# A bidirectional recurrence on one Trainium2 core: norms of the next unit in a thread of their own, block inverses of both directions merged together

## The chip, the cores and the metric

The kernel runs on one core of one Trainium2 chip. The metric is the device time of one execution in microseconds (us), lower is better. The kernel before takes 1797.82 us (median of 3 runs, 1797.66 to 1800.14).

## The reference

A small encoder trunk of one layer is applied to two requests (batches b = 0 and 1) of 512 tokens and 1024 features, in float32. The layer adds to x the sum of two gated branches, A (a bidirectional RWKV-7 recurrence of 8 heads of 64) and B (a latent attention of 8 heads), and then a SwiGLU block; a norm ends it. What the change touches is branch A, and in it the recurrence and the unit norm of kk:

```python
def _rwkv7_scan(r, w, k, v, kk, a, reverse):
    ...
    def step(state, inp):
        r_t, w_t, k_t, v_t, kk_t, a_t = inp
        sa = jnp.einsum('bhvk,bhk->bhv', state, kk_t)
        state = (state * w_t[:, :, None, :]
                 - sa[..., None] * (kk_t * a_t)[:, :, None, :]
                 + v_t[..., None] * k_t[:, :, None, :])
        return state, jnp.einsum('bhvk,bhk->bhv', state, r_t)
...
def _rwkv7_branch(p, w2, w0, a2, a0, g2, k_k, k_a, r_k, gn_g, gn_b):
    ...
    kk = heads(pk * k_k)
    kk = kk / jnp.maximum(jnp.sqrt(jnp.sum(kk * kk, axis=-1, keepdims=True)), 1e-12)
    ...
    o = (_rwkv7_scan(r, heads(wf), heads(kf), v, kk, heads(af), reverse=False)
         + _rwkv7_scan(r, heads(wb), heads(kb), v, kk, heads(ab), reverse=True))
    ...
    bonus = jnp.sum(r * heads(pk) * r_k, axis=-1, keepdims=True) * v
    return (o + bonus.reshape(bsz, s, A_WIDTH)) * g
```

The two requests share all weights.

## The kernel before

The recurrence isn't run token by token. The tokens are cut into 8 chunks of 64 (NCH, CH), and the work into 8 units: one per batch and pair of heads, in the order of `order` (pair 0 of batch 0, pair 0 of batch 1, pair 1 of batch 0 and so on). A unit treats both directions (NI = 2, the backward one on reversed tokens) and passes these steps:

- **prep**, first half (L822 and following): loads r, k and v in one tile (x3, L826), scales k to kk (L829), squares it (L831), sums the squares per head by a product (`row_stats`), takes the power -1/2 on POOL (L838, rn), spreads the result by `bcast_rows` (an ACT copy and four transposes) and forms nkk, the negated unit vectors (L842), and the bonus bo (L844 to L849, with the product bp). These are the norms. Then for each direction it loads decay and rate (c_, a_), scans, and forms pp, bt and kt.
- **prep**, second half: waits until the state run two units earlier is issued (`yield free`, since its buffers exist for two units), forms ka and kb, the products gx (L893, L894) and their masked copies nt and arb (L897, L898), and stores nt to HBM. It calls **lanes**, then makes the products gy and three groups of transposes per direction (tb, tk, vp).
- **lanes** (L938 to L971): inverts the 32x32 diagonal blocks of all chunks, heads and directions at once, by 31 dependent steps of a multiply (L963, lt) and an add (L965, el) on POOL, from a tile `lane` that is read back from HBM. The result goes to HBM (e_d).
- **merge** (L974 to L1004): joins the 32-blocks to 64-blocks. For each direction it loads e and ntl, transposes (L988, tp), multiplies (zp), copies (L995, z), multiplies (xp) and copies into e (L1003). The second direction follows the first.
- **state** (L1006): 8 dependent chunk steps, each with the products s1, s2 and s3 and between them copies to rs (L1033, DVE), sva (L1052, ACT), svb (L1053, DVE) and sums (L1060, L1061).
- **post** (L1066): copies o out (L1072), normalizes per head and stores y.

The order of TensorE's instructions is written by `drive`: threads of generators, each with an offset that is its priority. `drive` always resumes the first thread in the list that is due, and adds the modelled cost of its matmuls to a clock, `pe["now"]`. A yielded number asks for a pause of that many us of TensorE's clock, times SLACK (or SLS for the state thread); a yielded function waits until it is true. The offset is also the priority by which the other engines' instructions are ordered. The threads, first to last, are state, post, merge, prep, fill and combine. The prep thread does the units one after the other; merge i waits for a due time, TL us after lanes i was issued. Fill is the work that takes what is left of TensorE: the projections of r, k and v for the later pairs (pj_rkv), the gates (pj_gt, pj_gtl), and then the whole attention (sc, pt, pav, kps, qps, vps). Combine of batch 0 (pab) starts when all units and the attention of batch 0 are through. After that come the output projection, the combine of batch 1 and the SwiGLU block.

The short names of rows: lt and el are lanes, tp, z and zp, xp are merge, s is any of s1 to s3.

Of the kernel before, what the change touches and what calls it, by code (L numbers as in the profile page):

```python
# [18 lines left out]
P = 128  # L19
# [25 lines left out]
TL = 40  # L45
SLACK = 1.4
SLS = 1.2
# [12 lines left out]
YG = 0.75  # L60
YT = 1.43
YT2 = 0.85
YM1 = 2
YM2 = 1.1
YO1 = 1.3
# [3 lines left out]
YQ = 2.27  # L69
YK = 1.71  # L70
OFFS = 200000, 150000, 120000, 100000, 0, 0
# [9 lines left out]
PL = 4.06  # L81
# [26 lines left out]
def trunk(ctx, tc, outs, x, w_in, w2, g2, w_uq, w_ukk, w_ukv, w_oab, w_out, w_gu, w_down,  # L108
# [76 lines left out]
    def bcast_rows(sp, pp, rn, nh, name, rbtag):  # L185
# [624 lines left out]
    class Unit:  # L810
# [8 lines left out]
        def tmp(self, name):  # L819
            return rp0.tile([P, S], F32, tag="tmp", bufs=NT, name=f"{name}{self.nm}")  # L820

        def prep(self, free):  # L822
            b, p, nm, tmp = self.b, self.p, self.nm, self.tmp
            kra, krb, arb, bka, bkb = [], [], [], [], []
            x3 = rp0.tile([P, 3, S], F32, tag="rkv", bufs=1, name=f"rkv{nm}")
            nc.sync.dma_start(x3, rwkv_in[b][p][:, 0:3])  # L826
            r_, k_, v_ = x3[:, 0], x3[:, 1], x3[:, 2]
            kk = tmp("kk")
            nc.scalar.activation(kk, k_, AF.Copy, scale=cc(C_KK + p))  # L829
# [4 lines left out]
            ss = row_stats(_MG(), sq, 2, f"kk{nm}")  # L834
# [4 lines left out]
            rb = bcast_rows(rp0, _MG(), rn, 2, f"kk{nm}", ("tmp", NT))  # L839
            yield YP3  # L840
            nkk = rp0.tile([P, S], F32, tag="nkk", bufs=1, name=f"nkk{nm}")
            nc.vector.scalar_tensor_tensor(out=nkk, in0=kk, scalar=-1.0, in1=rb, op0=ALU.mult, op1=ALU.mult)  # L842
            bo = tmp("bo")
            nc.vector.scalar_tensor_tensor(out=bo, in0=r_, scalar=cc(C_RK + p), in1=k_, op0=ALU.mult, op1=ALU.mult)  # L844
            bp = mg(f"bp{nm}")
            mm(bp, b64, bo)
            yield YP4
            nc.vector.tensor_mul(bo, bp, v_)
            nc.sync.dma_start(bo_d[b][p], bo)  # L849
            halves = []  # L850
# [27 lines left out]
            for d, (rev, pp_, bt_, kt_) in enumerate(halves):  # L878
# [24 lines left out]
                kra.append(ka_), krb.append(kb_), arb.append(rb_)  # L903
            self.lanes()
# [69 lines left out]
        def merge(self):  # L974
            nm = self.nm
            nt, ed = nt_d[self.par], e_d[self.par]
            self.ee = []
            for i in range(NI):
                e_ = rp.tile([P, NCH, CH], F32, tag="e", bufs=4, name=f"e{nm}{i}")

                def tmp3(name):
                    return rp.tile([P, NCH, 32], F32, tag=name, bufs=1, name=f"{name}{nm}{i}")
                tp, ntl, z_ = tmp3("tp"), tmp3("ntl"), tmp3("z")
                for h, hs in enumerate((HA, HB)):
                    q = slice((i * 2 + h) * NCH, (i * 2 + h + 1) * NCH)
                    nc.sync.dma_start(ntl[Q[2 * h]], nt[q, 0:32, 32:].rearrange("c r t -> r c t"))
                    nc.sync.dma_start(e_[hs], ed[q].rearrange("c r t -> r c t"))
                nc.vector.transpose(tp, e_[:, :, 0:32])  # L988
                zp = mg(f"zp{nm}{i}").rearrange("p (c t) -> p c t", t=32)
                for c in range(NCH):  # L990
                    for h in range(2):
                        mm(zp[Q[2 * h + 1], c], ntl[Q[2 * h], c], tp[Q[2 * h], c], tile_position=(h * 64, h * 64 + 32))
                yield YM1
                for h in range(2):
                    (nc.scalar.copy, nc.vector.tensor_copy)[h](z_[Q[2 * h + 1]], zp[Q[2 * h + 1], 0:NCH])  # L995
                xp_ = mg(f"xp{nm}{i}").rearrange("p (c t) -> p c t", t=32)
                for c in range(NCH):
                    for h in range(2):
                        mm(xp_[Q[2 * h], c], z_[Q[2 * h + 1], c], e_[Q[2 * h + 1], c, 32:],
                           tile_position=(h * 64 + 32, h * 64))  # L1000
                yield YM2
                for h in range(2):
                    (nc.scalar.copy, nc.vector.tensor_copy)[h](e_[Q[2 * h], :, 32:], xp_[Q[2 * h], 0:NCH])  # L1003
                self.ee.append(e_)  # L1004
# [89 lines left out]
    def has(*k):  # L1094
        return lambda: k in done

    preps = [u.prep(has("state", i - 2) if i > 1 else 0 if i else "rp") for i, u in enumerate(units)]

    def first_prep():
        for r in preps[0]:  # L1100
            if r == "rp":
                return
            yield r
# [122 lines left out]
    drive(list(zip(OFFS, (state_thread(), post_thread(), merge_thread(), prep_thread(), fill_thread(),  # L1226
# [618 lines left out]
```

## Time and profile before

| | |
|---|---|
| runs | 1797.82 us median, 1797.66 to 1800.14 (3 runs) |
| the profiled execution | 1794.72 us |
| its span | 1792.9 us |
| mean granted TensorE clock | 0.985 |

The span goes from the first to the last instruction of the one profiled execution. Busy time is the time in which an engine worked (DMA issues and waits aren't counted); the idle time of an engine is followed by what ended it. PE is TensorE's matmuls, PEld its weight loads, which run beside them; DVE, ACT and POOL are the vector, scalar and general engines, SP issues most DMAs. In a stretch's row stand its bounds, its length, and for each engine the busy us and the instructions in it, then the granted clock of TensorE (1.00 is full speed), the share of the DMA engines and GB/s. In a row of waits stand the waiting instruction, the one it waited for, the total, the number of waits and the longest. Matmuls of an fp32 product are recorded as two passes, so that their count is twice that in the code.

### The profile page before, as it was taken

To read this page: it belongs to the slowest core of one execution; us is meant where nothing else is said; L and a number is where in the kernel's file an instruction comes from. 1 tells how busy PE (TensorE), PEld (TensorE's weight loads), DVE (VectorE), ACT (ScalarE), POOL (GpSimd) and SP (SyncE) were. 2 spreads that over 40 slices of the span, in tenths; PEclk is the share of its full clock that TensorE was granted. 3 is DMA by queue.
4 is the path that set the end of the run, shared out by engine and by line. 5 is a ranking of instruction groups with operands and counts; after the bars stand their busy time and mean duration, and the time that the engine had idled before them with its cause. 6 is when DMAs were issued, how large, how long until landed. Compare 5 with 4: busy or idle time off the path is not lost.

```text
span 1792.9 us, 30793 instructions
## 1 busy us (share of the span) xinstructions
PE 1706.5 (95%) x11660; PEld 1350.2 (75%) x11660; DVE 1076.8 (60%) x1781; ACT 786.1 (44%) x1525; POOL 625.9 (35%) x984
## 2 busy tenths in 40 slices
PE   7999999999999997999999999699999999989997
PEld 6778767777777775666667988488888888868886
DVE  6734564636445365855566657865565565498757
ACT  6743424344433336676663324333333333245445
POOL 1121536364553636260012126733343333200006
PEclk9999999999999998999999999799999999999999
DMA  5473343434334344211367531123222222283442
GB/s 179 140 254 100 114 112 81 128 92 119 114 85 121 86 113 118 73 39 34 129 200 265 177 114 36 36 87 107 94 90 99 83 88 77 100 300 116 131 134 95
DMA packets 185333, 208.97 MB, mean 117 GB/s; under 512 B 102816, under 2 KB 114464, under 8 KB 185184
## 3 DMA queue, kind: packets, MB, share of 16 engines
q1 hardware_dynamic: 184320, 205.48, 36.2%
q8 instruction: 92, 1.51, 0.4%
q10 hardware_dynamic: 720, 0.98, 0.2%
q0 software_dynamic: 144, 0.52, 0.1%
q14 instruction: 57, 0.47, 0.1%
HBM read 147.70 MB, written 59.24 MB: 115 GB/s over the span
## 4 chain that ended last, share of the span: by engine, by line
PE 69%; POOL 8%; DVE 8%; DMA 7%; issue 3%; ACT 2%; SPq 1%; POOLq 0%; DVEq 0%; ACTq 0%
PE pgC L128 10%; PE pgB L128 7%; PE pgA L128 6%; PE pj_gt L128 6%; PE dx L128 5%; PE pj_rkv L128 4%; PE pwo L128 4%; PE pab L128 4%; POOL el L965 3%; POOL lt L963 3%; PE dy L128 3%; PE sc L128 2%; PE s L128 2%; PE pj_mla L128 2%; PE pav L128 2%
## 5 line engine op out<-in xcount | busy, mean ns | idle before, releaser
L963 POOL TENSOR_TENSOR lt<-lane,el 128x126 f32<-128x126 f32 (+22 forms) x248 | 94.1, 379 | 37.1 <-DMA lane<-nt_d 18.6
L965 POOL TENSOR_TENSOR el<-el,lt 128x126 f32<-128x126 f32 (+22 forms) x248 | 96.7, 390 | 19.0
L128 PE MATMUL pj_gt<-h_lo,whi_gt 128*128 128x512 f32 x240 | 99.4, 414 | 0.0
L128 PE MATMUL pj_gt<-h_hi,wlo_gt 128*128 128x512 f32 x240 | 98.6, 411 | 0.9 <-DVE wlo_gt L136 0.9
L128 PE MATMUL pj_gt<-h_hi,whi_gt 128*128 128x512 f32 x240 | 99.0, 412 | 0.0
L128 PE MATMUL pab<-yo,wab 128*128 128x512 f32 x384 | 91.9, 393 | 2.9 <-DVE g L1178 1.4
L128 PE MATMUL pwo<-woh,m 128*128 128x256 f32 x512 | 93.6, 283 | 0.0
L128 PEld LDWEIGHTS pab<-yo,wab 128*128 128x128 f32 x384 | 70.8, 188 | 19.9 <-DVE wab L136 2.1
L1335 POOL TENSOR_TENSOR s<-uraw 128x512 f32<-128x512 f32 x22 | 29.2, 1328 | 150.9 <-DMA uraw<-in_w_gu 150.9
L128 PEld LDWEIGHTS pwo<-woh,m 128*128 128x128 f32 x512 | 80.2, 192 | 0.3
L128 PE MATMUL pj_rkv<-h_hi,wlo_rkv 128*128 128x512 f32 x192 | 78.7, 410 | 0.1
L128 PE MATMUL pj_rkv<-h_hi,whi_rkv 128*128 128x512 f32 x192 | 78.1, 407 | 0.0
L128 PE MATMUL pj_rkv<-h_lo,whi_rkv 128*128 128x512 f32 x192 | 77.7, 405 | 0.0
L128 PE MATMUL pwo<-wol,m 128*128 128x256 f32 x256 | 72.3, 284 | 0.5 <-DVE wol L136 0.5
L1714 POOL TENSOR_TENSOR x<-x,dp 128x512 f32<-128x512 f32 x4 | 6.3, 1591 | 177.4 <-DVE x L1713 177.4
L1403 DVE TENSOR_TENSOR p<-p,pgC 128x512 f32<-128x512 f32 x22 | 15.1, 687 | 83.6 <-PE pgC L128 83.6
L1180 POOL TENSOR_TENSOR g<-g 128x512 f32<-128x512 f32 x16 | 24.8, 1547 | 104.3 <-DVE g L1178 88.0
L1052 ACT COPY sva<-s 64x128 f32<-64x128 f32 x64 | 16.5, 257 | 98.5 <-PE s L128 87.9
L1053 DVE COPY svb<-s 64x128 f32<-64x128 f32 x64 | 18.9, 295 | 59.5 <-ACT sva L1052 37.9
L774 DVE TENSOR_REDUCE mx<-sc 128x1 f32<-128x512 f32 x64 | 43.7, 688 | 15.9 <-PE sc L128 14.9
L128 PEld LDWEIGHTS pj_gt<-h_hi,wlo_gt 128*128 128x128 f32 x240 | 45.1, 188 | 10.1 <-DVE wlo_gt L136 1.9
L128 PEld LDWEIGHTS pj_gt<-h_hi,whi_gt 128*128 128x128 f32 x240 | 45.1, 188 | 8.8
(1562 smaller groups left out, 5489.8 us busy)
## 6 DMA issues: line engine op xcount, KB each, us to landing
graw<-in_w_gu SPq DMA_DIRECT2D x22, 512.0 KB, 3.5
uraw<-in_w_gu SPq DMA_DIRECT2D x22, 512.0 KB, 3.5
a_d<-a SPq DMA_DIRECT2D x21, 512.0 KB, 3.3
w<-in_w_down SPq DMA_DIRECT2D x42, 256.0 KB, 4.7
x<-in_x SPq DMA_DIRECT2D x16, 512.0 KB, 7.2
rwkv_in<-lut SPq DMA_DIRECT2D x32, 256.0 KB, 2.4
gate_d<-gtt SPq DMA_DIRECT2D x32, 256.0 KB, 2.4
wab<-in_w_oab SPq DMA_DIRECT2D x32, 256.0 KB, 3.8
```

The costliest lines, as they stand in the source:

```text
L128: pin(nc.tensor.matmul(out, lhsT, rhs, start=start, stop=stop, **kw), n if out.shape[0] > 64 else n / 2)
L774: nc.vector.tensor_reduce(mx, sc, axis=AX.X, op=ALU.min)
L963: eng.tensor_mul(lv, lane[:, s, s + 1:].unsqueeze(1).to_broadcast([P, m_, n]), el[:, 0:m_, s].unsqueeze(2).to_broadcast([P, m_, n]))
L965: eng.tensor_add(ev, ev, lv)
L1052: nc.scalar.copy(sva[HA, :, c], s2[HA])
L1053: nc.vector.tensor_copy(svb[HB, :, c], s2[HB])
L1180: nc.gpsimd.tensor_add(g_[:, 0], g_[:, 0], g_[:, 1])
L1335: vg(ES[min(j, 1)]).tensor_add(s1, a21, a22)
L1403: nc.vector.tensor_add(p1, p1, x_)
L1714: nc.gpsimd.tensor_add(xs(1, t, 1), xs(1, t, 1), p5[t])
```

## The change

- The norms leave `prep` and become a generator of their own, `norms`, which loads k alone first (into a buffer that it shares with the rate tile a_), then r and k, then v. Square takes the scale k_k itself, so that kk is no longer formed; the sign comes in through `bcast_rows`; nkk is formed from k. The product for bo stands one pause ahead of its matmul, and the pause after it (YP4) is gone.
- A thread `norm_thread`, placed between prep and fill with an offset of 90000, runs the norms of unit i as soon as the lanes of unit i-1 are issued and r, k and v of the pair are there, after a pause YN. `prep_thread` waits for the norms of its unit.
- `prep` waits for the merge of the unit before (`lanes_free`) ahead of `lanes`, because `merge` now works in a buffer with the tag of `lane`.
- `merge` treats both directions in one go: one group of loads, two transposes, one product tile zp, two copies of twice the width, one product tile xp, and the copies into e. The pauses YM1 and YM2 come once per unit.
- Constants of the order are other: TL 44 for 40, SLACK 1.36 for 1.4, SLS 1.5 for 1.2, YG, YT, YM1, YO1, YQ and PL as shown.

```diff
-TL = 40
-SLACK = 1.4
-SLS = 1.2
+TL = 44
+SLACK = 1.36
+SLS = 1.5
...
-YG = 0.75
-YT = 1.43
+YG = 0.81
+YT = 1.82
...
-YM1 = 2
+YM1 = 1.55
...
-YO1 = 1.3
+YO1 = 1.02
...
-YQ = 2.27
+YQ = 2.53
...
+YN = 1
+EB = 4
+OFFS = 200000, 150000, 120000, 100000, 90000, 0, 0
...
-PL = 4.06
+PL = 4.5
...
-        nc.scalar.copy(rb, rn.rearrange("p (t h) -> p t h", t=4).unsqueeze(3).to_broadcast([P, 4, nh, P // nh]))
+        nc.scalar.mul(rb, rn.rearrange("p (t h) -> p t h", t=4).unsqueeze(3).to_broadcast([P, 4, nh, P // nh]), sign)
...
-        def prep(self, free):
+        def norms(self):
+
             b, p, nm, tmp = self.b, self.p, self.nm, self.tmp
-            kra, krb, arb, bka, bkb = [], [], [], [], []
-            x3 = rp0.tile([P, 3, S], F32, tag="rkv", bufs=1, name=f"rkv{nm}")
-            nc.sync.dma_start(x3, rwkv_in[b][p][:, 0:3])
-            r_, k_, v_ = x3[:, 0], x3[:, 1], x3[:, 2]
-            kk = tmp("kk")
-            nc.scalar.activation(kk, k_, AF.Copy, scale=cc(C_KK + p))
-            sq = tmp("kksq")
-            nc.scalar.activation(sq, kk, AF.Square)
+            kq = rp0.tile([P, S], F32, tag="a", bufs=1, name=f"kq{nm}")
+            nc.sync.dma_start(kq, rwkv_in[b][p][:, 1])
+            nc.scalar.activation(kq, kq, AF.Square, scale=cc(C_KK + p))
+            rk = rp0.tile([P, 2, S], F32, tag="rk", bufs=1, name=f"rk{nm}")
+            nc.sync.dma_start(rk, rwkv_in[b][p][:, 0:2])
+            v_ = rp0.tile([P, S], F32, tag="v", bufs=2, name=f"v{nm}")
+            nc.sync.dma_start(v_, rwkv_in[b][p][:, 2])
             yield F0 if Unit.first else YP1
...
             yield YP3
...
-            yield YP4
             nc.vector.tensor_mul(bo, bp, v_)
             nc.sync.dma_start(bo_d[b][p], bo)
+            self.rkv = r_, k_, v_, nkk
+
+        def prep(self, free, lanes_free):
...
+            yield lanes_free
             self.lanes()
...
+            w = rp.tile([P, 32, 32], F32, tag="lane", bufs=1, name=f"mrg{nm}").rearrange("p a b -> p (a b)")
+            tp = w[:, 0:S].rearrange("p (i c t) -> p i c t", i=NI, c=NCH)
+            nz = w[:, S:].rearrange("p (i c t) -> p i c t", i=NI, c=NCH)
...
+                nc.vector.transpose(tp[:, i], e_[:, :, 0:32])
+                self.ee.append(e_)
+            zp = mg(f"zp{nm}").rearrange("p (i c t) -> p i c t", i=NI, c=NCH)
...
+            yield YM1
+            for h in range(2):
+                (nc.scalar.copy, nc.vector.tensor_copy)[h](nz[Q[2 * h + 1]], zp[Q[2 * h + 1]])
...
+            yield YM2
+            for i in range(NI):
                 for h in range(2):
...
+                    (nc.scalar.copy, nc.vector.tensor_copy)[h](self.ee[i][Q[2 * h], :, 32:], xp_[Q[2 * h], i])
...
+    preps = [u.prep(has("state", i - 2) if i > 1 else 0 if i else "rp", has("merge", i - 1) if i else 0) for i, u in enumerate(units)]
...
+    def norm_thread():
+        for i, (_, p) in enumerate(order):
+            if i:
+                yield has("rkv", p)
+                yield has("lanes", units[i - 1].nm)
+                yield YN
+                yield from norms[i]
+            done.add(("norm", i))
+
     def prep_thread():
-        for i, (_, p) in enumerate(order):
-            yield has("rkv", p)
+        for i in range(NU):
+            yield has("norm", i)
             yield from preps[i]
             done.add(("prep", i))
```

More of the change, by code (lines that the diff above doesn't have):

```diff
@@ L838, in prep @@
             nc.gpsimd.tensor_tensor(rn, rn, mhalf[:, :8], op=ALU.pow)
-            rb = bcast_rows(rp0, _MG(), rn, 2, f"kk{nm}", ("tmp", NT))
+            rb = bcast_rows(rp0, _MG(), rn, 2, f"kk{nm}", ("tmp", NT), -1.0)
+            r_, k_ = rk[:, 0], rk[:, 1]
+            bo = tmp("bo")
+            nc.vector.scalar_tensor_tensor(out=bo, in0=r_, scalar=cc(C_RK + p), in1=k_, op0=ALU.mult, op1=ALU.mult)
             yield YP3
             nkk = rp0.tile([P, S], F32, tag="nkk", bufs=1, name=f"nkk{nm}")
-            nc.vector.scalar_tensor_tensor(out=nkk, in0=kk, scalar=-1.0, in1=rb, op0=ALU.mult, op1=ALU.mult)
-            bo = tmp("bo")
-            nc.vector.scalar_tensor_tensor(out=bo, in0=r_, scalar=cc(C_RK + p), in1=k_, op0=ALU.mult, op1=ALU.mult)
+            nc.vector.scalar_tensor_tensor(out=nkk, in0=k_, scalar=cc(C_KK + p), in1=rb, op0=ALU.mult, op1=ALU.mult)
             bp = mg(f"bp{nm}")
             mm(bp, b64, bo)
-            yield YP4
             nc.vector.tensor_mul(bo, bp, v_)
             nc.sync.dma_start(bo_d[b][p], bo)
+            self.rkv = r_, k_, v_, nkk
+        def prep(self, free, lanes_free):
+            b, p, nm, tmp = self.b, self.p, self.nm, self.tmp
+            r_, k_, v_, nkk = self.rkv
+            kra, krb, arb, bka, bkb = [], [], [], [], []
             halves = []
@@ L983, in merge @@
-                tp, ntl, z_ = tmp3("tp"), tmp3("ntl"), tmp3("z")
+                e_ = rp.tile([P, NCH, CH], F32, tag="e", bufs=EB, name=f"e{nm}{i}")
                 for h, hs in enumerate((HA, HB)):
                     q = slice((i * 2 + h) * NCH, (i * 2 + h + 1) * NCH)
-                    nc.sync.dma_start(ntl[Q[2 * h]], nt[q, 0:32, 32:].rearrange("c r t -> r c t"))
                     nc.sync.dma_start(e_[hs], ed[q].rearrange("c r t -> r c t"))
-                nc.vector.transpose(tp, e_[:, :, 0:32])
@@ L989, in merge @@
[L989 removed]
+                    nc.sync.dma_start(nz[Q[2 * h], i], nt[q, 0:32, 32:].rearrange("c r t -> r c t"))
+                nc.vector.transpose(tp[:, i], e_[:, :, 0:32])
+                self.ee.append(e_)
+            zp = mg(f"zp{nm}").rearrange("p (i c t) -> p i c t", i=NI, c=NCH)
+            for i in range(NI):
                 for c in range(NCH):
                     for h in range(2):
[L992 removed]
@@ L993, in merge @@
[L993 to L996, printed above, removed]
+                        mm(zp[Q[2 * h + 1], i, c], nz[Q[2 * h], i, c], tp[Q[2 * h], i, c],
+                           tile_position=(h * 64, h * 64 + 32))
+            yield YM1
+            for h in range(2):
+                (nc.scalar.copy, nc.vector.tensor_copy)[h](nz[Q[2 * h + 1]], zp[Q[2 * h + 1]])
@@ L997, in merge @@
+            xp_ = mg(f"xp{nm}").rearrange("p (i c t) -> p i c t", i=NI, c=NCH)
+            for i in range(NI):
                 for c in range(NCH):
                     for h in range(2):
-                        mm(xp_[Q[2 * h], c], z_[Q[2 * h + 1], c], e_[Q[2 * h + 1], c, 32:],
+                        mm(xp_[Q[2 * h], i, c], nz[Q[2 * h + 1], i, c], self.ee[i][Q[2 * h + 1], c, 32:],
                            tile_position=(h * 64 + 32, h * 64))
-                yield YM2
+            yield YM2
@@ L1002, in merge @@
+            for i in range(NI):
                 for h in range(2):
-                    (nc.scalar.copy, nc.vector.tensor_copy)[h](e_[Q[2 * h], :, 32:], xp_[Q[2 * h], 0:NCH])
-                self.ee.append(e_)
+                    (nc.scalar.copy, nc.vector.tensor_copy)[h](self.ee[i][Q[2 * h], :, 32:], xp_[Q[2 * h], i])
         def state(self):
@@ L1095, in has @@
         return lambda: k in done
-    preps = [u.prep(has("state", i - 2) if i > 1 else 0 if i else "rp") for i, u in enumerate(units)]
+    preps = [u.prep(has("state", i - 2) if i > 1 else 0 if i else "rp", has("merge", i - 1) if i else 0) for i, u in enumerate(units)]
+    norms = [u.norms() for u in units]
     def first_prep():
+        yield from norms[0]
         for r in preps[0]:
```

10 lines of the change are left out of this document (3 added, 7 removed).

## Prediction

> **What bounds the kernel now.** I read four views in this order: the page's first part, the busy time by stretches, TensorE's waits, and the timeline of one unit. First the page:
>
> ```profile
> span 1792.9 us, 30793 instructions
> ...
> PE 1706.5 (95%) x11660; PEld 1350.2 (75%) x11660; DVE 1076.8 (60%) x1781; ACT 786.1 (44%) x1525; POOL 625.9 (35%) x984
> ```
>
> TensorE is busy 95% of the span, and no other engine comes near. The change touches only the part with the recurrence, which runs from about 140 us to 972 us (the latter is where combine of batch 0 is through). Stretches of that part, each with its length, the busy times of PE, PEld, DVE, ACT, POOL, the granted clock and the DMA:
>
> ```profile
> 140.00:260.00 120.00, 115.88 (x776) 91.55 (x776) 65.80 (x113) 45.09 (x83) 43.52 (x95) 0.96 0.39 113
> 260.00:660.00 400.00, 390.44 (x4050) 289.09 (x4052) 205.00 (x427) 158.46 (x332) 202.69 (x463) 1.00 0.38 105
> 660.00:740.00 80.00, 67.88 (x684) 47.70 (x682) 49.15 (x97) 47.40 (x108) 39.44 (x87) 0.94 0.36 98
> 740.00:880.00 140.00, 134.25 (x1354) 93.59 (x1354) 85.23 (x181) 88.58 (x208) 41.62 (x95) 1.00 0.15 39
> 880.00:940.00 60.00, 57.61 (x285) 40.18 (x284) 39.71 (x63) 40.16 (x88) 8.40 (x6) 1.00 0.67 231
> 940.00:972.00 32.00, 29.41 (x125) 22.57 (x124) 22.95 (x32) 12.68 (x22) 7.64 (x5) 1.00 0.81 269
> ```
>
> Length minus PE gives TensorE's idle time: 4.1, 9.6, 12.1, 5.8, 2.4 and 2.6 us, together 36.5 us. The change leaves the number and shape of the matrix products as they are, so all it can win or lose is within this idle time and the clock. What TensorE waited for in the same 832 us (total, times, longest):
>
> ```profile
> PE s L128 <- DVE svb L1053: 12.4, 14, 3.6
> PE xp L128 <- DVE z L995: 4.1, 4, 2.2
> PE kps L128 <- ACT wkh L135: 3.9, 1, 3.9
> PE s L128 <- DVE rs L1033: 3.3, 5, 1.1
> PE bp L128 <- DVE bo L844: 2.1, 2, 1.3
> PE pab L128 <- DVE g L1178: 1.4, 1, 1.4
> PE pab L128 <- ACT wab L135: 1.1, 2, 0.7
> ```
>
> The state steps (svb, rs) make 15.7 us of it, the merge (xp after z) 4.1, the norms (bp after bo) 2.1, the start of the attention (kps) 3.9, the combine (pab) 2.5.
>
> Now the chain of a unit, from the timelines of POOL, ACT and DVE, in order of time (start, duration, engine, line):
>
> ```profile
> 277.26 0.43 POOL L963 TENSOR_TENSOR lt<-lane,el 128x31 f32<-128x31 f32 x1 [3.81 <-DMA lane<-nt_d]
> 298.73 0.75 ACT L807 COPY svb<-vp 64x256 f32<-64x256 f32 x2
> 310.30 0.23 POOL L965 TENSOR_TENSOR el<-el,lt 128x16 f32<-128x16 f32 x1
> 313.06 0.17 DVE L837 TENSOR_SCALAR rn<-ss_kk 128x8 f32<-128x8 f32 x1
> 317.90 0.45 DVE L988 STREAM_TRANSPOSE tp<-e 128x256 f32<-128x256 f32 x1 [4.67 <-DMA e<-e_d]
> 322.69 0.67 DVE L848 TENSOR_TENSOR bo<-bp,rkv 128x512 f32<-128x512 f32 x1
> 337.21 0.42 DVE L1003 COPY e<-xp 32x256 f32<-32x256 f32 x1
> 339.72 0.28 DVE L1033 COPY rs<-s 128x128 f32<-128x128 f32 x1
> 355.98 0.24 POOL L963 TENSOR_TENSOR lt<-lane,el 128x31 f32<-128x31 f32 x1 [1.97 <-DMA lane<-nt_d]
> L1072 ACT COPY os<-o x8: 577/587/593, 307.8 to 866.4; 128x512 f32<-128x512 f32 x8
> ```
>
> POOL solves unit 1 from 277.3 to 310.5 (33 us) and starts unit 2 at 356.0: 78.7 us from unit to unit. In between, unit 1's preparation ends at 299.5, and only then come unit 2's norms: the row sums reach DVE at 313.1, and bo at 322.7; 24 us of the cycle are norms. Beside them runs unit 1's merge, from tp at 317.9 to the last e at 337.6, direction after direction; state 1 begins at 339.7. The last row (the copy of o that ends a unit's states, first and last) gives (866.4 - 307.8) / 7 = 79.8 us per unit.
>
> So the chain is long, but TensorE fills it with other products. How much it has to fill shows in the rows of pj_gt (first whole, then the stretch 500 to 580), pj_rkv and pj_gtl, the projections that the fill thread runs until the attention, and in the stretch's own row:
>
> ```profile
> 185.00:940.00 755.00, 203.04 (x720) 0.99 0.36 104
> 500.00:580.00 80.00, 51.27 (x183) 1.00 0.40 111
> 185.00:940.00 755.00, 106.51 (x393) 0.99 0.36 104
> 185.00:940.00 755.00, 14.95 (x48) 0.99 0.36 104
> 500.00:580.00 80.00, 78.31 (x812) 58.00 (x811) 38.84 (x83) 31.38 (x66) 40.61 (x94) 1.00 0.40 111
> ```
>
> In 80 us, 51.3 of 78.3 busy us are projections; a unit itself needs only some 27 us of TensorE. Projections total 324.5 us.
>
> **The change, part by part.** All prices are against the profiled execution, 1794.72 us with a span of 1792.9; the runs' median is 1797.82 (1797.66 to 1800.14), 3.1 above it, and I carry the sum over to the median.
>
> *The cycle, not on the end's path.* With norms of unit i+1 allowed once unit i's lanes are issued, the 24 us lie beside the preparation's second half. Preparation i then waits for state i-2 (free), as before. From there: a PB pause of 5 x 1.36, four products gx and the lane load, 26 us by an estimate from the rows' spacing; 33 us solve; about 17 us for store, load and the joined merge (27 us before, from 310.5 to 337.6, of which 7 were to tp). A state run takes 49 us (258.8 to 307.8), and SLS 1.5 for 1.2 adds 8 x 2.59 x 0.3 = 6: 55. Two units per 26 + 33 + 17 + 55 = 131 us, so 66 us per unit instead of 80, and the last state ends near 775 instead of 866. By itself this is worth nothing: while TensorE is the bound, projections and attention only move behind it. What it changes is which work stands beside which.
>
> *State waits.* L1 + L2 + L3 spaced by 1.5 instead of 1.2 give 0.17, 0.31 and 0.30 us more between dependent steps. 14 waits of svb less 0.31 each make 4.3; 5 of rs less 0.17 make 0.8. **-5 us**; bounds -12 (all gone but the 3.6 us one in the attention's start) and 0, since SLACK 1.36 instead of 1.4 shortens all other pauses a little.
>
> The rows of single steps that the next three parts use (min/median/max in ns, then the first and last start):
>
> ```profile
> L829 ACT ACTIVATE kk<-rkv,col x8: 722/722/726, 128.4 to 679.5; 128x512 f32<-128x512 f32 x8
> L838 POOL TENSOR_TENSOR rn<-rn,mhalf x8: 1647/1652/1654, 143.6 to 717.7; 128x8 f32<-128x8 f32 x8
> PE pj_gt L128 <- DVE wlo_gt L136: 0.9, 2, 0.6
> L995 ACT COPY z<-zp x16: 362/363/366, 239.9 to 816.2; 32x256 f32<-32x256 f32 x16
> L995 DVE COPY z<-zp x16: 429/429/431, 245.1 to 816.6; 32x256 f32<-32x256 f32 x16
> ```
>
> *Norms.* kk is gone: one ACT copy of 0.72 us per unit, with Square taking the scale itself, and the minus sign goes into the ACT copy of rb. Both lie off the path. bo's DVE product is now issued a pause before its matmul, so bp's wait goes: **-2 us**; bounds -2.1 and 0. Loads: k comes twice, three DMAs instead of one, on SP, which also carries the projections' weights; the queue waits for its buffers either way, and I price it 0, at most +2 (TensorE waited only 0.9 us in all for pj_gt's weight halves). The power op on POOL (1.65 us) now falls into the solve of the unit before; it lengthens that by 1.7 of 33 us, off the end's path.
>
> *Joined merge.* Sixteen waits become eight, but each copy of z moves 512 columns on 32 partitions instead of 256 (0.36 on ACT and 0.43 on DVE become some 0.6 and 0.7 by proportion) after a pause of 1.55 x 1.36 = 2.1 instead of 2.8 us. **-1 us**; bounds -4 and +3. lane, tp, ntl and z share one buffer now, so lanes(i+1) wait for merge i: covered, since state i-2 frees the preparation later than that.
>
> *A wait that moves.* tp stands in DVE's queue, and DVE stood idle 4.67 us before it. In the kernel before, no state ran then (307.8 to 339.7). With the shorter cycle merge i falls into state i-1, whose copies rs and svb queue behind tp on the same DVE, and TensorE waits for those. TL 44 instead of 40 puts the merge later by 4 us, about that idle time. **+2 us**; bounds 0 and +20 (below).
>
> *Start of the attention.* It comes when the projections are through. Unit work before it: at 66 us per unit about 7 units, so 185 + 324.5 + 7 x 27 + 12 idle = 710 us, not 680. By then state 6 has ended (707) and state 7 not begun (720): little is left to cover the attention's first loads. Before:
>
> ```profile
> 680.00:690.00 10.00, 5.96 (x54) 3.66 (x50) 5.34 (x11) 4.05 (x9) 8.90 (x17) 0.80 0.67 205
> 690.00:700.00 10.00, 6.06 (x64) 4.59 (x65) 7.18 (x16) 8.40 (x20) 8.67 (x19) 0.84 0.44 133
> ```
>
> 8 us idle in 20 and a clock of 0.8, with half of the busy time recurrence. Without it up to 6 us more are idle; on the other side ACT (8.4 of 10 busy) is freed of the unit's copies, which stand between the attention's casts. **+2 us**; bounds -6 and +6, and the clock goes with the idle time.
>
> *Tail.* The store that ends a unit's post, and the group of combine's products (both batches):
>
> ```profile
> L1087 SPq DMA_DIRECT2D y_d<-os x8: 319/323/1008, 328.2 to 882.2; - x8
> L128 PE MATMUL pab<-yo,wab 128*128 128x512 f32 x384 | 91.9, 393 | 2.9 <-DVE g L1178 1.4
> ```
>
> The combine of batch 0 may start when all units are through and attention 0 is. Before, that was 882 us, so it could fill only the last 50 us of the attention, and ran into its own loads at 940 to 972 (2.6 us idle). Now attention 0 decides, some 85 us after its start, near 800; combine's 46 us of products (half of 91.9) can fill gaps for 130 us (4% of idle time from 740 to 940), and its loads spread. **-4 us**; bounds -8 and 0.
>
> Sum: -5 - 2 - 1 + 2 + 2 - 4 = **-8 us**: 1786.7 in a profiled execution, 1789.8 as median.
>
> [...]
>
> **Rivals.**
> - *No change that counts* (0.17). TensorE is the bound and the waits only change places: state waits shrink, those of merge and attention start grow by as much. For it: every mechanism here is within 36.5 us of idle time. 1794 to 1801 as median.
> - *Slower: DVE blocked behind tp* (0.19). Place: L988's queue position in the middle of a state run. Price: units 1 to 7 stall by what DVE waits for e, at most 5.6 us in the rows and 3.1 in the mean, less the 0.8 us that a step's pause covers: 7 x 2.3 = 16 us instead of my +2, so -8 - 2 + 16 = +6: 1804. It decides once e lands over 1 us after DVE has come to tp while a state step is due; TL's 4 us speak against it, POOL's longer solve for it.
>
> ```profile
> DVE tp L988 <- DMA e<-e_d: 25.1, 8, 5.6
> ```
>
> - *The chain is the bound after all* (0.04). If TensorE's busy time were elastic, the 91 us by which the states end earlier would come off in part; half of it gives 1752. Against it: the 51 us of projections per 80.
> - *The overlap doesn't happen*, since rkv of the next pair is late or the order by due times puts the norms last: then the -5 and -2 remain. That lies within the forecast's own range.
>
> **How the numbers follow.** The forecast (0.60) has a range of its own of 1778 to 1794: the waits of state and tail at their better bounds (-8 - 4), and at the other end the sum at half. The range must leave out no more than 2 in 10: 1778 to 1804 leaves out the fourth case, half of the slower case and a little of the forecast's tail. A difference of 0.2% is 3.6 us, about what a measurement of this kernel tells from none. Faster: 0.60 + 0.04 = 0.64; within: 0.17; slower: 0.19.
>
> **What the changed profile would show.** Right: POOL's solves start some 66 us apart and the last os<-o near 775; norms stand before the end of the preparation before them; TensorE's waits for svb and rs fall to about 10 us, that for bo is gone; pab begins well before the attention's end; idle time of the part about 28 us. Wrong: the solves are still 79 us apart (no overlap); waits of s for rs or svb right after a tp with idle time before it (the slower rival); a stretch of over 12 us idle with a low clock where the attention starts; or a stage that ends far sooner than its idle time allows.

## The result, and the profile after

The changed kernel takes 1824.09 us (median of 4 runs, 1820.53 to 1824.6); the kernel before, run beside it, 1798.23 us (4 runs, 1797.66 to 1800.14). The ratio is 1.0155, with a 95% interval of 1.0135 to 1.0175: slower, outside the predicted range and on the other side of no change. The page of the changed kernel begins:

```profile
span 1822.6 us, 30792 instructions
...
PE 1711.1 (94%) x11660; PEld 1355.8 (74%) x11660; DVE 1080.2 (59%) x1773; ACT 779.8 (43%) x1509; POOL 659.7 (36%) x984
```

The span is 29.7 us longer. TensorE executes the same 11660 matmuls and is busy only 4.6 us longer, so most of the loss is idle time. POOL is busy 34 us longer with the same 984 instructions (625.9 before). The stretches of the part with the recurrence, with the columns as before:

```profile
140.00:260.00 120.00, 110.44 (x736) 87.62 (x735) 65.77 (x113) 44.65 (x81) 50.70 (x96) 0.94 0.42 120
260.00:660.00 400.00, 372.20 (x3949) 275.81 (x3942) 206.37 (x412) 149.46 (x314) 221.42 (x459) 0.97 0.37 102
660.00:740.00 80.00, 73.02 (x743) 53.92 (x738) 36.39 (x75) 27.06 (x58) 44.94 (x90) 0.96 0.29 79
740.00:880.00 140.00, 128.72 (x1279) 90.30 (x1278) 85.57 (x181) 87.10 (x207) 42.99 (x93) 0.94 0.23 60
880.00:940.00 60.00, 58.43 (x291) 40.50 (x290) 39.05 (x67) 45.44 (x104) 7.43 (x5) 1.00 0.60 213
940.00:1000.00 60.00, 59.21 (x288) 44.19 (x287) 37.08 (x58) 32.92 (x66) 8.94 (x6) 1.00 0.51 166
```

Length minus PE is TensorE's idle time: 9.6 (4.1 before in this stretch), 27.8 (9.6), 7.0 (12.1), 11.3 (5.8), and little behind 880 us. It is the middle of the units, 260 to 660 us, that loses, and its clock fell from 1.00 to 0.97. The whole part, from 140 us to the first product of the output projection (pwo), before and after:

```profile
140.00:972.00 832.00, 795.47 (x7266) 584.68 (x7266) 467.83 (x910) 392.37 (x841) 343.31 (x749) 0.99 0.38 110
140.00:1003.00 863.00, 804.24 (x7270) 593.85 (x7268) 472.46 (x905) 387.78 (x829) 377.17 (x749) 0.97 0.37 107
```

It ends at 1003.0 instead of 972.0 us, 31.0 us later, a little more than the whole loss of the span. Idle time grew from 36.5 to 58.8, so 22.2 us of it; the other 8.8 are products taking longer (outside the part TensorE is busy 4.2 us less). By what comes next on TensorE, the idle time ahead of products of the state steps (s and o) grew from 16.8 to 32.3, ahead of merge products from 4.1 to 8.0, and ahead of the attention from 7.8 to 8.1. The waits, from 140 to 1000 us:

```profile
PE s L130 <- DVE svb L1066: 10.7, 13, 1.6
PE s L130 <- DVE svb L1074: 9.7, 8, 2.0
PE s L130 <- DVE rs L1046: 6.2, 10, 1.8
PE zp L130 <- issue: 6.0, 1, 6.0
PE o L130 <- DVE svb L1066: 5.7, 3, 3.0
PE kps L130 <- ACT wkh L137: 3.9, 1, 3.9
```

The state's rows (svb twice, rs, and o after svb) make 32.3 us, where before svb and rs made 15.7: doubled, where the prediction took 5 away. The wait of zp stands at 247.5 us, in the first unit's merge; bp's wait for bo is gone, and that of kps is unchanged.

**The cycle.** The last copy of a unit (os<-o) for all 8 units, and then the chain from the end of one unit's states over the solve that starts at 514 us (all 31 of POOL's lt, and its last el) to the end of the states two units later:

```profile
L1085 ACT COPY os<-o x8: 580/586/588, 324.0 to 868.8; 128x512 f32<-128x512 f32 x8
480.55 0.59 ACT L1085 COPY os<-o 128x512 f32<-128x512 f32 x1 [2.15 <-PE o L130]
L972 POOL TENSOR_TENSOR lt<-lane,el x31: 227/407/1182, 514.2 to 554.5; 128x126 f32<-128x126 f32 x3, 128x30 f32<-128x30 f32 x2, 128x56 f32<-128x56 f32 x2, 128x78 f32<-128x78 f32 x2
554.86 0.63 POOL L974 TENSOR_TENSOR el<-el,lt 128x16 f32<-128x16 f32 x1
581.25 0.29 DVE L1046 COPY rs<-s 128x128 f32<-128x128 f32 x1 [0.77 <-PE s L130]
640.90 0.59 ACT L1085 COPY os<-o 128x512 f32<-128x512 f32 x1
```

(868.8 - 324.0) / 7 = 77.8 us per unit, against 79.8 before and 66 forecast. The norms do lie where the change puts them: bo of the fourth unit ends at 375.1 us, in the third unit's solve. But every link of the chain came out longer than forecast. From one os to the next solve of that pair of buffers 480.55 to 514.2 = 33.7 us; solve 514.2 to 555.5 = 41.3; from there to the first rs 25.7; state run 581.25 to 640.9 = 59.7. Together 160.4 us for two units, where the prediction added 26 + 33 + 17 + 55 = 131.

**What made the solve longer.** The same solve in the kernel before, and then all 248 lt and el of the eight solves, before and after:

```profile
L963 POOL TENSOR_TENSOR lt<-lane,el x31: 225/367/912, 514.5 to 547.0; 128x126 f32<-128x126 f32 x3, 128x30 f32<-128x30 f32 x2, 128x56 f32<-128x56 f32 x2, 128x78 f32<-128x78 f32 x2
```

```profile
L963 POOL TENSOR_TENSOR lt<-lane,el 128x126 f32<-128x126 f32 (+22 forms) x248 | 94.1, 379 | 37.1 <-DMA lane<-nt_d 18.6
L965 POOL TENSOR_TENSOR el<-el,lt 128x126 f32<-128x126 f32 (+22 forms) x248 | 96.7, 390 | 19.0
```

```profile
L972 POOL TENSOR_TENSOR lt<-lane,el 128x126 f32<-128x126 f32 (+22 forms) x248 | 111.1, 448 | 49.1 <-DMA lane<-nt_d 28.3
L974 POOL TENSOR_TENSOR el<-el,lt 128x126 f32<-128x126 f32 (+22 forms) x248 | 113.5, 458 | 18.2
```

The instructions are the same and each takes 0.07 us more in the mean, 33.8 us in all. The timeline of the changed kernel shows which ones; a DVE scan beside the add at 454.58, and at 461 two DVE products with two inputs beside the state's own two products on POOL (sp, a part of each state step):

```profile
454.11 0.39 POOL L972 TENSOR_TENSOR lt<-lane,el 128x110 f32<-128x110 f32 x1
454.21 1.38 DVE L866 TENSOR_TENSOR_SCAN c<-rst,c 128x512 f32<-128x512 f32 x1 [1.61 <-DMA c<-rwkv_in]
454.58 1.20 POOL L974 TENSOR_TENSOR el<-el,lt 128x110 f32<-128x110 f32 x1
...
460.70 0.85 DVE L877 TENSOR_TENSOR kt<-kt,c 128x512 f32<-128x512 f32 x1
460.97 0.84 POOL L1057 TENSOR_TENSOR sp<-sva,pc 64x128 f32<-64x128 f32 x1
461.48 0.88 DVE L138 TENSOR_TENSOR wlo_gt<-wraw_gt,whi_gt 128x512 fp32r<-128x512 f32 x1
461.85 0.26 ACT L1065 COPY sva<-s 64x128 f32<-64x128 f32 x1 [1.09 <-POOL sp L1057]
461.89 0.74 POOL L1058 TENSOR_TENSOR sp<-svb,pc 64x128 f32<-64x128 f32 x1
462.66 0.29 DVE L1066 COPY svb<-s 64x128 f32<-64x128 f32 x1 [0.30 <-POOL sp L1058]
463.01 0.27 PE L130 MATMUL s<-sva,bka 128*64 128x64 f32 x1 [1.62 <-DVE svb L1066]
```

The add of 0.4 us takes 1.20; the two sp of 0.4 us (median of 56 each) take 0.84 and 0.74 and are late, svb behind them, and TensorE waits 1.62 us. Of the 496 products and adds of the solves, 142 overlap in time with a DVE instruction with two inputs from SBUF (below: "beside DVE work"), and these are 46.0 us longer in all than the shortest of their shape; the other 354 only 1.3 us. In the kernel before it is 59, with 12.5 us, and 2.2 us for the rest. The sums tie the excess to the overlap; by what means the overlap lengthens them isn't shown. The waits for sp from 255 to 880 us, before and after (the waiting instruction, total, times, longest):

```profile
DVE svb L1053 <- POOL sp L1045: 11.0, 7, 2.3
ACT sva L1052 <- POOL sp L1044: 6.0, 6, 1.9
```

```profile
ACT sva L1065 <- POOL sp L1057: 31.6, 16, 5.7
DVE svb L1066 <- POOL sp L1058: 23.8, 18, 2.8
```

**What made the products longer, in part.** Stretches of 2 us around one wait of TensorE (of 1.92 us, that of zp at 566.6 us):

```profile
564.00:566.00 2.00, 2.00 (x21) 1.38 (x20) 0.00 (x0) 0.39 (x1) 0.00 (x0) 1.00 1.36 193
566.00:568.00 2.00, 0.57 (x3) 0.14 (x1) 0.00 (x1) 0.23 (x1) 0.00 (x0) 1.00 1.18 209
568.00:570.00 2.00, 1.36 (x54) 1.23 (x56) 1.58 (x6) 0.00 (x0) 1.36 (x1) 0.74 0.31 114
570.00:572.00 2.00, 2.00 (x34) 1.91 (x30) 1.01 (x2) 1.21 (x2) 0.29 (x1) 0.50 0.18 48
...
574.00:576.00 2.00, 2.00 (x27) 1.37 (x28) 0.30 (x1) 0.00 (x0) 0.34 (x1) 0.55 0.50 131
576.00:578.00 2.00, 2.00 (x60) 1.78 (x54) 0.73 (x2) 1.39 (x3) 0.00 (x0) 1.00 0.04 8
```

After the wait the granted clock stands at 0.50 for some 7 us, and the 128x512 products of pj_gt start 0.43 us apart (572.90, 573.33, 573.75) instead of 0.23 (562.88, 563.11, 563.35 us). An estimate from these figures is that the wait of 1.9 us costs some 3 us more in slower products. Between 180 and 1000 us the kernel before has three such episodes, with gaps of 2.2 to 3.9 us; the changed one has eight, with gaps of 1.4 to 6.0 us. In the part, the time at half clock grew from 20.5 to 58.0 us. That this makes all of the 8.8 us isn't shown: two variants below have 58.0 us at half clock as well (mean granted clock 0.975 in all three), and their products take 3.3 us (TL 51) and 11.2 us longer (norms after the preparation, new constants).

### The profile page after: what moved, and what is told of

Same layout as the page of the kernel before. It is cut to its first block, busy times and chain, and to the rows that moved or that the text cites. A ratio compares the mean times of both kernels' runs of the same rounds, so it can differ in the third digit from the quotient of the medians.

```text
span 1822.6 us, 30792 instructions
## 1 busy us (share of the span) xinstructions
PE 1711.1 (94%) x11660; PEld 1355.8 (74%) x11660; DVE 1080.2 (59%) x1773; ACT 779.8 (43%) x1509; POOL 659.7 (36%) x984
## 4 chain that ended last, share of the span: by engine, by line
PE 62%; POOL 12%; DMA 8%; DVE 8%; issue 4%; SPq 2%; ACT 2%; POOLq 0%; DVEq 0%; ACTq 0%
PE pgC L130 10%; PE pgB L130 6%; PE pgA L130 6%; PE dx L130 5%; POOL lt L972 4%; PE pj_rkv L130 4%; POOL el L974 4%; PE pwo L130 4%; PE pab L130 3%; PE dy L130 3%; PE pj_gt L130 2%; PE pj_mla L130 2%; PE sc L130 2%; PE gx L130 2%; PE dz L130 1%
## 5 line engine op out<-in xcount | busy, mean ns | idle before, releaser
L972 POOL TENSOR_TENSOR lt<-lane,el 128x126 f32<-128x126 f32 (+22 forms) x248 | 111.1, 448 | 49.1 <-DMA lane<-nt_d 28.3
L974 POOL TENSOR_TENSOR el<-el,lt 128x126 f32<-128x126 f32 (+22 forms) x248 | 113.5, 458 | 18.2
L130 PE MATMUL pj_gt<-h_hi,whi_gt 128*128 128x512 f32 x240 | 103.4, 431 | 0.0
L1428 DVE TENSOR_TENSOR p<-p,pgC 128x512 f32<-128x512 f32 x22 | 15.1, 687 | 83.5 <-PE pgC L130 83.5
L130 PEld LDWEIGHTS pj_gt<-h_lo,whi_gt 128*128 128x128 f32 x240 | 46.4, 194 | 9.4 <-issue 1.2
```

The lines of the kernel that those rows point to most:

```text
L130: pin(nc.tensor.matmul(out, lhsT, rhs, start=start, stop=stop, **kw), n if out.shape[0] > 64 else n / 2)
L972: eng.tensor_mul(lv, lane[:, s, s + 1:].unsqueeze(1).to_broadcast([P, m_, n]), el[:, 0:m_, s].unsqueeze(2).to_broadcast([P, m_, n]))
L974: eng.tensor_add(ev, ev, lv)
L1428: nc.vector.tensor_add(p1, p1, x_)
```

## The experiments

Six statements could explain the loss: the norms in their own thread, the joined merge, the constants, POOL slowed by DVE, DVE's queue ahead of the state copies, and the order of TensorE as such. That order is written by a model in which only matmuls, pauses and conditions count, so a changed pause or thread writes another order, and an instruction moved between other engines doesn't. Below, "state idle" is TensorE's idle time ahead of s and o (before 16.8, after 32.3), and "later" is how much later than in the kernel before the part ends, as idle time plus the rest (after 31.0 = 22.2 + 8.8; rounded, so that sums can be 0.1 off). All ratios are to runs of the kernel before on the same chip. Ratios are of all executions, the other figures of the one that was profiled; it was 6 to 10 us shorter than the median with the new constants alone (1820.86), with TL 41 (1810.35) and without YP4 (1808.48), so that there "later" falls short of the ratio.

**The parts, with old constants.** First the changed kernel with all constants that the change sets anew put back (TL 40, SLACK 1.4, SLS 1.2 and so on):

```diff
-TL = 44
-SLACK = 1.36
-SLS = 1.5
+TL = 40
+SLACK = 1.4
+SLS = 1.2
...
```

> The changed structure (norms in a thread, joined merge) with all the old constants of the order. Crowding theory (the norms and first half of the next unit's preparation now lie beside a state run, on the same DVE and POOL that the state steps need): still slow, 1812 to 1826 us, POOL's solve still about 41 us instead of 33. Constants theory (the other pauses cost the time): back to 1795 to 1801. Merge theory (the joined merge stalls TensorE): slow as well, 1812 to 1826.

1861.97 us, ratio 1.0369 (1.0339 to 1.04); state idle 39.8; 62.1 later = 42.3 + 19.8. Its waits name the state first:

```profile
PE s L130 <- DVE svb L1066: 17.7, 15, 2.6
PE o L130 <- DVE svb L1066: 9.7, 4, 3.4
```

Then the new constants alone, in the kernel before:

```diff
-TL = 40
+TL = 44
...
```

> The kernel before with nothing but the new constants (TL, SLACK, SLS, YG, YT, YM1, YO1, YQ, PL). Crowding theory and merge theory: 1793 to 1804. Constants theory: 1815 to 1825.

1830.86 us, ratio 1.019 (1.0158 to 1.0222); state idle only 8.4, but 25.5 later = 19.5 + 6.0, with 11.8 us of idle time ahead of the combine and 11.3 ahead of merge products. With all the new constants the state waits do fall, as the prediction said of the wider steps, and the time went to other waits.

The joined merge alone (old constants, and norms of a unit only after the preparation before it):

```diff
-                yield has("lanes", units[i - 1].nm)
-                yield YN
+                yield has("prep", i - 1)
```

> The joined merge in the shared buffer and the norms as a function of their own, but each unit's norms start only when the preparation before is issued, as in the kernel before; old constants. Crowding theory: 1790 to 1803, TensorE's waits for svb and rs at 16 us as before. Merge theory: 1812 to 1826 with waits at zp and after tp. Constants theory: 1795 to 1801.

1824.71 us, ratio 1.0168 (1.0151 to 1.0185); state idle 20.5; 27.1 later = 23.9 + 3.2. The thread of norms with the merge put back to direction after direction, still in the shared buffer, old constants:

```diff
-            zp = mg(f"zp{nm}").rearrange("p (i c t) -> p i c t", i=NI, c=NCH)
+                zp = mg(f"zp{nm}{i}").rearrange("p (c t) -> p c t", t=32)
...
-            xp_ = mg(f"xp{nm}").rearrange("p (i c t) -> p i c t", i=NI, c=NCH)
+                xp_ = mg(f"xp{nm}{i}").rearrange("p (c t) -> p c t", t=32)
```

> The norms in their thread, but the merge direction after direction as before (in the shared buffer, so that lanes still wait for it); old constants. Crowding theory: slow, 1808 to 1826. Merge theory: back to 1793 to 1803. Constants theory: 1795 to 1801.

1866.43 us, ratio 1.0394 (1.0372 to 1.0415); state idle 36.0; 70.1 later = 46.2 + 23.8. So with old constants the thread costs 1861.97 - 1824.71 = 37 us. The joined merge comes out 4 us better by the first and the fourth of these, but their intervals overlap. Each such pair compares two written orders as well as two structures.

**Single suspects in the changed kernel.** POOL's two state products on DVE, with TensorE's order in this part as it was:

```diff
-                    nc.gpsimd.tensor_mul(sp_[HA], sva[HA, :, c], pcb[HA])
-                    nc.gpsimd.tensor_mul(sp_[HB], svb[HB, :, c], pcb[HB])
+                    nc.vector.tensor_mul(sp_[HA], sva[HA, :, c], pcb[HA])
+                    nc.vector.tensor_mul(sp_[HB], svb[HB, :, c], pcb[HB])
```

> The changed kernel with the two products sp of a state step on DVE instead of POOL. Late-POOL theory (beside the next unit's preparation POOL is slower and has more queued, so that sp comes late and the state copies wait for it): TensorE's idle time ahead of state products falls from 32 us to 15 to 20 and the time from 1824 to 1802 to 1812. DVE-queue theory (the copies come late because DVE itself is full of preparation): no gain or a loss, 1820 to 1830.

1831.69 us, ratio 1.020 (1.0169 to 1.0232); state idle 37.8. Taking sp off POOL saves nothing: DVE has the backlog of the preparation, and sp stands in that queue instead (from 255 to 880 us ACT's copy of sva waits 16.3 us for sp on DVE in three waits, 7.0 the longest). The preparation's first half after the wait for the state run (all units but the first):

```diff
+            if nm != "00":
+                yield free
             kra, krb, arb, bka, bkb = [], [], [], [], []
```

> The changed kernel, with the wait for the state run two units back moved ahead of the first half of a unit's preparation (norms stay early; unit 0 as it was). Crowding theory (the scans and products of the first half beside a state run and a POOL solve do the harm): POOL's solve back from 41 to 33 to 36 us, state idle time back to about 18 us, 1800 to 1812 us. If the first half isn't the cause: 1822 or more, since the chain of a unit gets longer.

1820.49 us, ratio 1.0141 (1.0101 to 1.0181), inside the changed kernel's own interval. It settles nothing: the edit moved the place in the program, but DVE's preparation still ran beside the solve (152 products of the solve beside DVE work, 142 in the changed kernel). The changed kernel with norms after the preparation, new constants kept (the edit of the third experiment):

> The changed kernel with all its constants, but each unit's norms start only when the preparation before is issued. Crowding theory: POOL's solve at 33 us and few state waits, 1800 to 1815 us, faster than the changed kernel. If the norm thread itself is worth something with these constants, slower than 1824. Against the joined merge with old constants (1825) it shows what the constants do for the merge alone.

1826.63 us, ratio 1.0172 (1.0144 to 1.02); state idle 5.7, and 46 products of the solve beside DVE work, fewer than before the change. And still 29.9 later = 18.7 + 11.2, with waits at other places:

```profile
PE gx L130 <- DVE arb L906: 8.8, 6, 2.6
PE ss_gn L130 <- ACT osq L1092: 7.9, 6, 2.9
PE xp L130 <- DVE mrg L1007: 6.2, 6, 3.1
```

(Of these three the kernel before has only xp's, 4.1 us, and the changed one 0.3 and 0.8 us of the first two.) This kernel has no overlap of norms, no contention beyond that of before, short state waits, and loses as much. With the new constants the thread therefore costs nothing (1.0155 with it, 1.0172 without). Its counterpart, sp on DVE in the kernel before (the edit of the fifth), with the written order unchanged:

> The kernel before with the two products sp on DVE. Late-POOL theory: a small gain, since there DVE and ACT waited only 17 us for sp in all, 1786 to 1796 us. DVE-queue theory: 1798 to 1806.

1797.57 us, ratio 1.0014 (0.9999 to 1.0028). In an order that fits, the state's products may stand in either engine's queue.

**How little it takes.** Norms after the preparation, merge direction after direction and old constants: what is left of the change is that kk isn't formed, three loads for one, the pause YP4 gone, and the shared buffer:

```diff
-            yield YP4
...
+            yield lanes_free
...
+            w = rp.tile([P, 32, 32], F32, tag="lane", bufs=1, name=f"mrg{nm}").rearrange("p a b -> p (a b)")
```

> Norms after the preparation before, merge direction after direction (in the shared buffer), old constants: what is left of the change are the dropped kk, the three loads for one, and the buffer. If the joined merge is what costs 30 us with old constants (1825): 1793 to 1804. If the split norms, their loads or the shared buffer cost it: 1815 to 1828.

1828.2 us, ratio 1.0178 (1.0163 to 1.0193); 30.0 later = 17.1 + 12.9; 62 products beside DVE work. The third experiment, with the joined merge, is 3.5 us shorter, again with intervals that overlap (1.0151 to 1.0185 there). The joined merge alone with a later merge:

```diff
-TL = 40
+TL = 47
```

> The joined merge alone with old constants, but TL 47 for 40, so that TensorE comes to zp 7 us later by its own clock. If the merge costs time because TensorE reaches zp before both directions' e and transposes are there: merge idle time from 18 to under 8 us, 1803 to 1815. If the joined merge does its harm elsewhere (its wider copies, the queue of DVE): 1820 to 1830.

1828.42 us, ratio 1.0185 (1.017 to 1.0201): the idle time ahead of merge products went from 18.5 to 0, and that ahead of post (12.5) and preparation (9.9) took its place. The kernel before with nothing but wider state steps:

```diff
-SLS = 1.2
+SLS = 1.5
```

> The kernel before with only SLS 1.5 for 1.2. The prediction's step on state waits (-5 us by itself): TensorE's idle time ahead of state products from 17 to 8 to 12 us, 1787 to 1794. If the constants only work together: 1797 to 1812, with the idle time come back at other places.

1821.56 us, ratio 1.0142 (1.0122 to 1.0161); state idle 14.4, above the 8 to 12 expected; 23.3 later = 9.7 + 13.6. So wider steps alone take only 2.4 us off the state idle. The changed kernel with a later merge:

```diff
-TL = 44
+TL = 51
```

> The changed kernel with TL 51 for 44, nothing else. Blocked-behind-tp theory (DVE reaches the transposes before e has landed, and state copies and zp wait behind): the waits at zp (7.9 us) and those of state copies behind a transpose (some 5 us) go, with the half-clock stretches after them, 1806 to 1815. If the waits on POOL's sp and on DVE's backlog of preparation are the main thing: 1819 to 1828.

1835.06 us, ratio 1.0216 (1.0201 to 1.0231); state idle 39.8. A still later merge is no cure. The next three are nudges of the kernel before, and the fourth keeps its order:

```diff
-TL = 40
+TL = 41
```

> The kernel before with one constant moved by 2.5%: the merge's due time TL 41 instead of 40; no instruction is added or removed, and TensorE's order is the same up to the first merge. Theory A (before's written order is a finely fitted one, and any other order that the same rules write loses some 25 to 36 us): 1812 to 1830 us, idle time of TensorE from 140 us to combine's end over 45 us against 36.4, clock deficit over 17 us against 10.3. Theory B (the losses seen so far come each from its own item, such as SLS 1.5 or the shared lane buffer, and a nudge of this size does nothing): 1793 to 1802 us.

```diff
-SLACK = 1.4
+SLACK = 1.41
```

> The kernel before with all pauses but those of the state run longer by 0.7% (SLACK 1.41 for 1.4). Theory A (fitted order): 1812 to 1830 us. Theory B (own items): 1793 to 1802 us.

```diff
-            yield YP4
```

> The kernel before without the pause YP4 ahead of the second part of the norms, the one pause that the change takes away: the units' preparation comes 2.84 x 1.4 = 4 us earlier. Theory A (fitted order): 1812 to 1830 us. Theory B (own items): if this pause is the item behind the loss of the kernel with serial norms and a merge direction after direction, 1815 to 1830 as well, while the two other nudges stay at 1793 to 1802; if not, 1790 to 1802.

```diff
-            nc.sync.dma_start(x3, rwkv_in[b][p][:, 0:3])
+            for j in (1, 0, 2):
+                nc.sync.dma_start(x3[:, j], rwkv_in[b][p][:, j])
```

> The kernel before with the unit's load of r, k and v cut into three loads, k first; TensorE's written order is the same. Theory A (it is the order that costs): 1794 to 1802 us. Theory B (the additional loads are one of the items): 1803 to 1825 us, with waits of the norms for rkv that the kernel before does not show.

| | median us | ratio (95%) | later = idle + rest |
|---|---|---|---|
| TL 41 | 1816.48 | 1.0111 (1.0088 to 1.0135) | 12.6 = 4.3 + 8.4 |
| SLACK 1.41 | 1800.13 | 1.0029 (1.0018 to 1.0039) | 3.1 = 2.5 + 0.6 |
| no YP4 | 1814.7 | 1.0102 (1.0078 to 1.0126) | 15.1 = 7.8 + 7.4 |
| three loads | 1794.99 | 0.9993 (0.9977 to 1.0009) | 0.7 = -1.5 + 2.3 |

The strong form of "any other order loses 25 to 36 us" falls: SLACK 1.41 costs 5 us, the two others some 20. The form that stands: another written order of this kernel cost something every time it was tried (nine kernels without the overlapping norms, 5 to 36 us; five of them change only constants or a pause), while the two edits that leave the order of the kernel before alone (three loads, sp on DVE) cost nothing.

**Contention with the order kept.** svb's copy taken out of DVE's queue:

```diff
-                nc.vector.tensor_copy(svb[HB, :, c], s2[HB])
+                nc.scalar.copy(svb[HB, :, c], s2[HB])
```

> The changed kernel with the copy of svb on ACT instead of DVE; TensorE's written order in the part with the recurrence stays as it is. Theory A (DVE's queue, with the preparation ahead of svb, carries the state waits): TensorE's waits for svb, 26 us in the changed kernel, fall below 10, its idle time ahead of state products from 32 to about 20, and the time to 1808 to 1815 us. Theory B (the loss sits in the written order as a whole, and what one queue gains comes back at another wait): 1818 to 1832 us.

1828.55 us, ratio 1.0177 (1.0159 to 1.0195). The wait only changed its name: in place of 16.4 us for svb on DVE (10.7 and 5.7)

```profile
PE s L130 <- ACT svb L1066: 9.7, 9, 2.8
PE s L130 <- DVE svb L1074: 9.1, 6, 2.4
PE s L130 <- DVE rs L1046: 8.4, 10, 2.7
```

State idle fell from 32.3 to 27.7 and nothing came of it. svb alone isn't the cause. At last, three products per direction of DVE's preparation are left out of the changed kernel, so that its results are other values and TensorE's order is the same:

```diff
-                nc.vector.tensor_mul(bt_, bt_, c_)
...
-                nc.vector.tensor_mul(kt_, kt_, rev(k_))
-                nc.vector.tensor_mul(kt_, kt_, c_)
```

> The changed kernel with three of the four in-place products per direction in the first half of prep left out (bt by c, kt by k, kt by c), so bt and kt hold other values; TensorE's written order is the same. That takes 6 products of 0.69 to 0.9 us per unit, some 36 us in all, off DVE, and with them work beside POOL's solve and the state copies. Theory A (DVE's preparation beside solve and state run makes the loss, at DVE and at POOL): idle time ahead of state products falls from 32 to about 20 us, the products of the solve beside DVE work from 142 to under 110, and the time to 1806 to 1815 us. Theory B (the written order as a whole): 1818 to 1828 us.

1810.32 us, ratio 1.0084 (1.0058 to 1.0111): 13.8 us off, about half of the loss. State idle 22.9, products of the solve beside DVE work 105 with 31.4 us excess, and POOL back near its old busy time:

```profile
PE 1710.3 (95%) x11660; PEld 1356.8 (75%) x11660; DVE 1047.4 (58%) x1725; ACT 779.5 (43%) x1509; POOL 635.4 (35%) x984
```

So the preparation's DVE work, where the changed kernel puts it, does cost TensorE time, over POOL and DVE's queue together. How much the same cut would bring in the kernel before was not run; there all state waits together are 16.8 us.

## Why the prediction was wrong

- **The step that failed** is in the paragraph on the cycle: "By itself this is worth nothing: while TensorE is the bound, projections and attention only move behind it. What it changes is which work stands beside which." The first of these sentences stands: with the old constants (first experiment) os runs from 316.3 to 838.3 us, which is 74.6 us per unit, a shorter cycle, and that kernel is some 38 us slower than the changed one. The last sentence named one cause, and only tp in DVE's queue (+2) and the power op (1.7 us of the solve, off the path) were priced of it. The links were carried over from the kernel before (solve 33, state run 49 and 6 for SLS), as if work put beside them left their durations alone. They came out at 41.3 and 59.7, so the cycle is 77.8 us and not 66, and the state waits beside them doubled. Argued from the trace, and borne out in part by the last experiment: DVE's two-input work moved into solve and state run (59 products of the solves beside it before, 142 after).
- **The bound.** That "all it can win or lose is within this idle time and the clock" holds for a gain alone: the idle time itself grew by 22.2 us.
- **State waits**, -5: they doubled, 15.7 to 32.3 us. With the new constants alone state idle is 8.4 us; with the wider SLS alone it is 14.4 against 16.8, and that kernel is 26 us slower.
- **The wait that moves and its rival.** The rival's pattern is there, in the timeline of DVE and TensorE (in the changed kernel's rows tp bears the name of the shared buffer, mrg):

```profile
477.92 0.45 DVE L997 STREAM_TRANSPOSE mrg<-e 128x256 f32<-128x256 f32 x1 [1.74 <-DMA e<-e_d]
479.17 0.45 DVE L997 STREAM_TRANSPOSE mrg<-e 128x256 f32<-128x256 f32 x1 [0.80 <-DMA e<-e_d]
479.64 0.29 DVE L1066 COPY svb<-s 64x128 f32<-64x128 f32 x1
479.99 0.27 PE L130 MATMUL o<-arb,svb 64*64 64x64 f32 x1 [2.99 <-DVE svb L1066]
```

  DVE waits twice for e, svb stands behind, and TensorE is idle for 2.99 us. It is one of the three waits of o for svb, 5.7 us in all, not the 16 that the rival asked for. The rival had the right sign and the wrong size, and TL doesn't mend it.
- **Norms**, -2: bp's wait went, and idle time ahead of all norms products went only from 2.2 to 1.6. **Merge**, -1: the two pairs of runs that differ in it (4 and 3.5 us) don't tell it from nothing, and in the changed kernel the idle time ahead of zp and xp rose from 4.1 to 8.0, 6.0 of it in one wait in the first unit.
- **Attention start**, +2: 7.8 to 8.1. **Tail**, -4: the last unit ends at 868.8 instead of 775, so combine of batch 0 couldn't start earlier; its idle time fell by 2.1.
- **What had no term at all**: that the order of TensorE fits the durations of the kernel before, as if it were tuned to them. A pause less, or TL 41, costs some 20 us there. The prediction costed edits one by one against the 36.5 us of idle time that this order leaves, with no term for a new order. And the products that take longer, 8.8 us, in part by the slower clock behind new gaps: the clock was mentioned only with the attention.

Settled: the loss doesn't need the joined merge (without it, it is 33 us and more), the additional loads cost nothing in the kernel before, and moving sp or the copy of svb to another engine doesn't mend it. Settled too that a new written order alone costs 5 to 36 us here, and that the thread costs 37 us more with old constants and nothing with the new ones. Open: how the changed kernel's loss divides between a worse fit and the contention of DVE and POOL, so that the cause of the whole is not shown. The two don't add up: without the overlap and with the new constants, the contention is gone and the loss is the same. The kernel before stayed the fastest that was run, level with its own two variants of the same order.

## What to carry to other kernels

When a kernel's order is written ahead by a model and fitted by constants, price a change first as a new order: nudge one constant of the old kernel by a few per cent and see what that costs, since a structural gain has to be larger to show. When work moves beside other work, don't carry durations over; look up in the trace what an instruction takes when the other engine is busy beside it (here 0.32 us more for each of POOL's 142), and use that in the chain. And where a bound engine loses its clock after short gaps (here 0.50 for 3.4 to 17.1 us), price a wait by its length and the slower stretch behind it.

## What the runs showed of the hardware

- POOL products and adds that take 0.22 to 0.46 us at the shortest took up to 1.4 us beside a two-input DVE instruction; on average 46.0 / 142 = 0.32 us more each. The other 354 of the changed kernel took 1.3 us more in all.
- TensorE's granted clock fell to 0.50 for 3.4 to 17.1 us at a time in the kernels before and after. Between 180 and 1000 us it fell there with every gap of TensorE of 2.2 us or more, with some of 1.4 to 2.0 us (1.39, 1.65, 1.90 and 1.92, but not 1.83 or 2.00), and with none below. The length of one gap doesn't decide it: of two gaps of 3.46 us ahead of dy, in the SwiGLU block, the one in the kernel before (ended at 1571.5 us) left the clock at 0.50 from 1571 to 1577 us, and the one in the changed kernel (ended at 1601.4 us) passed at 1.00. With svb on ACT a gap of 2.79 us (ended at 463.0 us) passed as well, the clock at 1.00 from 460 to 470 us.
